# A two-layer diffusion backbone: the pace at which gate projections are handed out inside windowed attention

## The chip, the cores and the metric

The kernel runs on one core of one Trainium2 chip. The metric is the device time of one execution in microseconds (us). Before the change it is 1504.61 us, the median of 3 runs (1503.4 to 1506.65). Engines are called by their names: TensorE (PE in the profile, with PEld for its weight loads), VectorE (DVE), ScalarE (ACT), GpSimd (POOL) and SyncE (SP), which issues the DMA transfers.

## The reference, cut to what matters

There are 1024 latent tokens and 256 context tokens of width 1024, and two layers. The change lies in the first layer, whose core is this:

```python
def even_layer(hl, hc, w_in, sink, ln_g, ln_b, w_s, b_s, w_out, row, col, need_ctx):
    q, k, v, u, vv, gate = jnp.split(hl @ w_in, EVEN_SPLITS, axis=-1)
    q = rope_2d(q.reshape(B_, S, A_HEADS, A_HEAD_DIM), row, col)       # 8 heads of 64
    k = rope_2d(k.reshape(B_, S, A_KV_HEADS, A_HEAD_DIM), row, col)    # 2 key/value heads
    ...
    a = windowed_sink_gqa(q, k, v, kc, vc, sink)   # window of 128, context keys, a sink logit
    b = chunk_gmlp(gelu(u), gelu(vv), ln_g, ln_b, w_s, b_s)
    y = (jnp.concatenate([a, b], axis=-1) * jax.nn.silu(gate)) @ w_out
    ...                                            # the same for the context tokens
```

After it the stream is x + gate_l * y, a norm follows, and the second layer (multi-head latent attention) begins. All matrix products of this kind are made as three matmuls of numbers split into a high and a low part.

## The kernel before, in words

The program computes tokens in blocks of 128 (8 latent blocks, then 2 context blocks: NT = 10), and projections in groups of 512, 512 and 256 tokens (GROUPS). In the first layer `layer0_in` makes queries and keys, then the values and the gMLP branch, and then two things at once:

- `attention0` is a generator over 20 units, each a block of 128 queries with one key/value head (4 query heads). The context blocks come first (two key blocks of 128), then latent blocks 0 to 7: these have three neighbouring key blocks (two at the ends, so units 4, 5, 18 and 19 have one less) and two context key blocks. It works as a pipeline over iterations n = 0 to 23, in the order of ORDER0 (line 48): `S0 S1 D Q M S2 S3 A1 D D A2 P HV HG S4 U D A3 X I F`. S are the scores of unit n, one key block each, with ScalarE's copy (line 712) and VectorE's running maximum (715, 717). M, P, HV, HG, X and F belong to unit n-1: transposes and reduction of the maximum (723, 725), its spread over the partitions (732, with ScalarE's copy mb, 737), the shift of the scores on VectorE and GpSimd (746, 744), the exponentials (752), their fold (761 to 765). A1, A2, U and A3 belong to unit n-2: P·V (774), in odd iterations the row sums (779), and the store (787 to 791). I inverts the sums of some blocks. At each D the generator yields.
- `dense` is a generator of steps of the gates' projections (eight blocks of 128 gate columns, times three token groups). A step is three chunks of K (nine matmuls) or the last two (six). Gate 7 on the latents is done in eight steps of one chunk for both groups, each freeing one tile h0_c, into which `load_wo` (637) then casts a row block of w_out0; before them `load_wo` has issued the loads. After that `gate_out` (563) applies SiLU (ScalarE's tanh, 185; VectorE, 186), multiplies by the gMLP branch (568) and stores to y_d (570).

At every yield of attention, the loop at 630 takes as many steps of `dense` as RATE asks for; PRE = 3 steps are taken ahead. All this stands in a section in which the order of TensorE, ScalarE, VectorE and GpSimd is the order of the program. SyncE's order is the framework's, and so is that of what comes later, which may be put between attention's instructions. Later comes `layer0_out`: for every block of 128 tokens `front` loads yf from y_d (859), the gate halves from ga_d and the inverses from r0_d, multiplies them (867, 868), casts them to yh and yl, and multiplies by w_out0 (881: tiles b<-h,yh, 48 matmuls of 512 columns); `back` normalises and transposes (901).

The loop that hands out the steps:

```python
for _ in range(PRE):
    next(steps)
for n, _ in enumerate(attention):
    while done < (n + 1) * RATE:
        next(steps, None)
        done += 1
for _ in steps:
    assert False
```

Of the kernel before, what the change touches and what calls it, by code (L numbers as in the profile page):

```python
# [25 lines left out]
EPS = 1e-6  # L26
NEG = -1e30
PTS = 3
RATE = 0.95
PRE = 3  # L30
XB = 8
ADA = ((), (), (3, 7), (3, 7), (3,))
# [21 lines left out]
class Kernel:  # L54
# [257 lines left out]
    def layer0_in(self):  # L312
# [311 lines left out]
        with self.tc.manual_schedule(engines={E.PE, E.Activation, E.DVE, E.Pool}):  # L624
# [5 lines left out]
# [3 lines that stand above are left out]
# [946 lines left out]
```

## Time and profile before

| what | value |
|---|---|
| median of 3 runs | 1504.61 us |
| profiled execution, its own time | 1504.3 us |
| its span from first to last instruction | 1502.5 us |
| TensorE busy in the span | 1439.6 us (96%) |
| VectorE busy | 879.5 us (59%) |
| ScalarE busy | 735.9 us (49%) |
| GpSimd busy | 397.4 us (26%) |
| first score matmul of the first layer's attention | 294.00 us |
| last gate matmul of the first layer | 492.55 us |
| first matmul of its output projection | 515.91 us |

In the timeline a row is: start in us, duration in us, engine, line of the kernel, operation, output<-inputs by the program's names, shapes, number of instructions merged into the row, and in brackets the idle time of that engine just before it with what ended it. TensorE's matmuls are pipelined, so rows overlap, and the cost of one in a stream is the distance from start to start. Helpers record their own lines: L100 to L102 are the three matmuls of any split product, L88 any cast on ScalarE, L96 any subtraction of a high part. What is meant shows in the tile names: b<-h,w_hi are gate projections on the latents, b<-h,yh the output projection.

### The profile page before, as it was taken

What the parts mean: (1) busy time and instruction counts of PE and PEld (TensorE: products, weight loads), DVE (VectorE), ACT (ScalarE), POOL (GpSimd) and SP (SyncE); (2) the same over time, 40 slices, a digit from 0 to 9 for tenths busy, and PEclk for the clock granted to TensorE, in tenths of its full rate; (3) what the DMA queues carried; (4) which work ended last, traced back from release to release, by engine and by line L of the source; (5) the groups of instructions that cost most, each with busy time, mean ns of one, the idle gap of its engine ahead of it and who ended that gap; (6) DMA issues with size and microseconds to landing.
All of it is one profiled execution on the core that took longest, in us unless ns stands there. A gap on an engine that the chain in (4) does not pass through costs nothing.

```text
span 1502.5 us, 23133 instructions
## 1 busy us (share of the span) xinstructions
PE 1439.6 (96%) x8849; PEld 1132.6 (75%) x8849; DVE 879.5 (59%) x1690; ACT 735.9 (49%) x1563; POOL 397.4 (26%) x351
## 2 busy tenths in 40 slices
PE   5999999999999799999998999999999999999998
PEld 3766899777666478879887777777777777776786
DVE  5582124356667877543745766676667666766454
ACT  4422310145567635443435766666666666676321
POOL 4243233223556533232470110011001100124100
PEclk9999999999999999999999999999999999999999
DMA  8557401222214646321231000000000000212241
GB/s 329 230 219 272 136 29 29 85 81 85 72 39 155 188 123 191 130 76 57 71 127 39 24 24 15 25 24 24 15 25 24 24 15 22 71 46 81 96 144 71
DMA packets 83783, 132.64 MB, mean 88 GB/s; under 512 B 7552, under 2 KB 59976, under 8 KB 80600
## 3 DMA queue, kind: packets, MB, share of 16 engines
q1 hardware_dynamic: 83528, 130.91, 25.9%
q8 instruction: 69, 1.13, 0.3%
q14 instruction: 42, 0.34, 0.1%
q10 hardware_dynamic: 144, 0.26, 0.0%
HBM read 99.59 MB, written 31.56 MB: 87 GB/s over the span
## 4 chain that ended last, share of the span: by engine, by line
PE 75%; DVE 9%; ACT 5%; issue 4%; DMA 4%; POOL 2%; SPq 0%; POOLq 0%; DVEq 0%; ACTq 0%
PE acc L1270 9%; PE tm L1252 7%; PE s L100 7%; PE s L101 7%; PE s L102 7%; PE b L100 5%; PE b L101 4%; PE b L102 4%; PE s L1215 3%; PE s L1216 3%; PE s L1217 3%; PE tm L100 2%; PE acc L774 2%; DVE peak L1227 2%; ACT prob L1242 2%
## 5 line engine op out<-in xcount | busy, mean ns | idle before, releaser
L1259 ACT COPY pt<-tm 128x512 f32<-128x512 f32 x192 | 112.4, 585 | 165.7 <-PE tm L1252 165.7
L1252 PE MATMUL tm<-ident,prob 128*128 128x128 f32 x1280 | 178.3, 273 | 7.8 <-ACT pt L1259 2.1
L1252 PEld LDWEIGHTS tm<-ident,prob 128*128 128x128 f32 x1280 | 150.8, 140 | 42.0 <-PE tm L1252 9.5
L1242 ACT ACTIVATE prob<-s,peak 128x1024 f32<-128x1024 f32 x128 | 143.3, 1120 | 38.0 <-DVE peak L1231 29.6
L1227 DVE TENSOR_REDUCE peak<-s 128x1 f32<-128x1024 f32 x128 | 155.0, 1211 | 1.8 <-PE s L1217 1.7
L1270 PE MATMUL acc<-pt,v 128*64 128x256 f32 x1280 | 152.0, 384 | 0.0
L96 POOL TENSOR_TENSOR ql<-pe,qh 32x512 fp32r<-32x512 f32 x32 | 40.7, 1271 | 413.2 <-ACT qh L88 386.2
L1261 DVE COPY pt<-tm 128x512 f32<-128x512 f32 x128 | 87.8, 686 | 79.4 <-PE tm L1252 77.4
L96 POOL TENSOR_TENSOR w_lo<-raw,w_hi 128x512 fp32r<-128x512 f32 (+1 forms) x60 | 74.9, 1261 | 199.0 <-DVE w_hi L90 98.5
L1270 PEld LDWEIGHTS acc<-pt,v 128*64 128x64 f32 x1280 | 86.3, 136 | 49.7 <-issue 9.6
L1215 PE MATMUL s<-kh,qh 96*128 96x512 f32 x256 | 109.2, 426 | 2.5 <-DVE raw L186 1.5
L1216 PE MATMUL s<-kl,qh 96*128 96x512 f32 x256 | 100.9, 394 | 0.0
L1217 PE MATMUL s<-kh,ql 96*128 96x512 f32 x256 | 100.8, 394 | 0.0
L1168 DVE TENSOR_TENSOR ql<-tm,qh 64x256 fp32r<-64x256 f32 x62 | 26.1, 421 | 83.7 <-ACT qh L1166 83.3
L100 PE MATMUL b<-h,yh 128*128 128x512 f32 x160 | 63.8, 399 | 3.7 <-ACT yh L88 2.7
L100 PE MATMUL s<-h,w_hi 128*128 128x512 f32 x160 | 63.9, 412 | 2.2 <-ACT qk L380 2.2
L101 PE MATMUL s<-h,w_hi 128*128 128x512 f32 x160 | 63.7, 398 | 0.3 <-DVE rs_v L125 0.3
L101 PE MATMUL b<-h,yh 128*128 128x512 f32 x160 | 63.3, 395 | 0.0
L102 PE MATMUL s<-h,w_lo 128*128 128x512 f32 x160 | 63.0, 395 | 0.0
L102 PE MATMUL b<-h,yl 128*128 128x512 f32 x160 | 62.5, 391 | 0.0
L1242 ACT ACTIVATE prob<-sx,peak 128x256 f32<-128x256 f32 x128 | 61.0, 477 | 0.6
L1217 PEld LDWEIGHTS s<-kh,ql 96*128 96x128 f32 x256 | 48.0, 188 | 11.2
(469 smaller groups left out, 3733.7 us busy)
## 6 DMA issues: line engine op xcount, KB each, us to landing
wa<-in_w_ada_dram SPq DMA_DIRECT2D x16, 1024.0 KB, 9.1
x<-in_xs_dram SPq DMA_DIRECT2D x20, 512.0 KB, 5.6
raw<-in_w_dram SPq DMA_DIRECT2D x17, 512.0 KB, 3.6
wa<-in_w_adag_dram SPq DMA_DIRECT2D x8, 1024.0 KB, 5.9
raw<-in_w_out_dram SPq DMA_DIRECT2D x10, 512.0 KB, 3.9
yf<-y_d SPq DMA_DIRECT2D x10, 512.0 KB, 5.6
x_d<-x SPq DMA_DIRECT2D x8, 512.0 KB, 4.5
raw<-in_w1g_dram SPq DMA_DIRECT2D x8, 512.0 KB, 3.4
```

What stands on the lines that cost most here:

```text
L96: e.tensor_tensor(lo, src, hi.bitcast(F32), op=ALU.subtract)
L100: mm(out, lhsT=ah, rhs=bh, start=start, stop=False)
L101: mm(out, lhsT=ah, rhs=bl, start=False, stop=False)
L102: mm(out, lhsT=al, rhs=bh, start=False, stop=stop)
L1215: mm(o, lhsT=qh[0:96, q], rhs=kh[0:96, k0:k1], start=True, stop=False)
L1216: mm(o, lhsT=qh[0:96, q], rhs=kl[0:96, k0:k1], start=False, stop=False)
L1217: mm(o, lhsT=ql[0:96, q], rhs=kh[0:96, k0:k1], start=False, stop=True)
L1227: nc.vector.reduce_max(m[:, 0, a:a + 1], banks[n, a], axis=AX.X)
L1242: nc.scalar.activation(probs[n][j][:, TL:T] if c else probs[n][j][:, 0:TL], src, AF.Exp, bias=peaks[n][:, 2, j:j + 1], scale=scale, accum_ ...
L1252: nc.tensor.transpose(tp[:, o * P:(o + 1) * P], probs[n][j][:, k * P:(k + 1) * P], self.ident)
L1259: nc.scalar.copy(dst, src)
L1270: mm(accs[m][64 * e:64 * e + 64, 0:QG], lhsT=self.v4[hp // 2][:, kt, vc:vc + 64], rhs=pts[2 * m + e][:, kt], start=kt == 0, stop=kt == NT - 1)
```

## The change

The constant that sets how many steps of `dense` are taken per yield of attention goes from 0.95 to 0.85. Nothing else differs.

```diff
@@ -26,7 +26,7 @@
 EPS = 1e-6
 NEG = -1e30
 PTS = 3
-RATE = 0.95
+RATE = 0.85
 PRE = 3
 XB = 8
 ADA = ((), (), (3, 7), (3, 7), (3,))
```

## Rows read from the trace of the kernel before

**Rows 1.** Windows: stretch, length, busy PE, PEld, DVE, ACT, POOL, clock, DMA share, GB/s.

```profile
360.00:380.00 20.00, 20.00 (x110) 13.96 (x107) 14.23 (x26) 12.77 (x26) 7.74 (x6) 1.00 0.23 75
...
480.00:500.00 20.00, 16.00 (x86) 10.29 (x86) 16.48 (x23) 17.44 (x31) 15.84 (x10) 1.00 0.28 84
500.00:520.00 20.00, 12.79 (x74) 7.67 (x71) 16.45 (x25) 9.40 (x18) 8.74 (x7) 0.91 0.70 223
520.00:540.00 20.00, 20.00 (x110) 15.31 (x109) 18.53 (x29) 11.33 (x22) 8.52 (x7) 1.00 0.48 137
```

**Rows 2.** TensorE's waits from 300 to 493.5: total us, times, longest us.

```profile
PE s L707 <- ACT pt L712: 3.2, 6, 1.1
PE s L723 <- DVE mx L717: 1.2, 2, 0.8
```

**Rows 3.** TensorE's waits from 493.5 to 516.

```profile
PE s L723 <- DVE mx L717: 4.0, 2, 2.6
PE b L100 <- ACT yh L88: 2.7, 1, 2.7
PE tm L732 <- DVE peak L726: 2.6, 1, 2.6
PE s L707 <- ACT pt L712: 0.7, 2, 0.5
```

**Rows 4.** Timeline of TensorE around the last gate step.

```profile
492.32 0.39 PE L101 MATMUL b<-h,w_hi 128*128 128x512 f32 x1
492.55 0.40 PE L102 MATMUL b<-h,w_lo 128*128 128x512 f32 x1
...
499.10 2.38 PE L774 MATMUL acc<-pt,vt 128*64 128x256 f32 x20
504.11 0.65 PE L732 MATMUL tm<-ident,peak 128*128 128x128 f32 x4 [2.63 <-DVE peak L726]
...
505.16 0.64 PE L779 MATMUL acc<-fold,ones 128*32 128x256 f32 x8
...
515.91 0.79 PE L100 MATMUL b<-h,yh 128*128 128x512 f32 x1 [2.74 <-ACT yh L88]
```

**Rows 5.** Windows of the hole, of its end, and of what follows.

```profile
493.05:515.91 22.86, 12.79 (x83) 6.74 (x81) 18.92 (x28) 14.08 (x26) 14.43 (x9) 1.00 0.59 187
512.50:515.91 3.41, 0.67 (x9) 0.15 (x3) 3.38 (x4) 1.10 (x2) 1.68 (x1) 1.00 1.09 372
...
515.91:519.33 3.42, 3.42 (x10) 2.56 (x10) 3.39 (x7) 0.89 (x2) 0.00 (x0) 0.50 0.93 262
```

**Rows 6.** Timeline of ScalarE in the hole.

```profile
495.65 2.27 ACT L752 ACTIVATE pt<-pt 128x512 f32<-128x512 f32 x4 [0.56 <-DVE pt L746]
...
498.77 1.09 ACT L185 ACTIVATE gg<-b 128x512 f32<-128x512 f32 x2
...
507.33 2.27 ACT L752 ACTIVATE pt<-pt 128x512 f32<-128x512 f32 x4 [0.32 <-DVE pt L746]
```

**Rows 7.** Timeline of VectorE: the gates' products and yf's.

```profile
500.23 1.35 DVE L568 SCALAR_TENSOR_TENSOR gg<-gg,ub 128x512 f32<-128x512 f32 x1
502.21 1.04 DVE L568 SCALAR_TENSOR_TENSOR gg<-gg,ub 128x512 f32<-128x512 f32 x1
...
512.37 0.69 DVE L867 SCALAR_TENSOR_TENSOR yf<-yf,raw 128x512 f32<-128x512 f32 x1 [3.27 <-DMA yf<-y_d]
513.09 1.64 DVE L868 TENSOR_TENSOR yf<-yf,raw 128x512 f32<-128x512 f32 x1
```

**Rows 8.** The chain of waits, 485 to 530: start, us, what.

```profile
506.28 5.97 DMA yf<-y_d
```

**Rows 9.** Timeline of TensorE: maxima of three units, one after the other.

```profile
445.96 0.60 PE L723 MATMUL s<-ident,mx 128*128 128x128 f32 x4
...
457.12 0.60 PE L723 MATMUL s<-ident,mx 128*128 128x128 f32 x4
...
468.63 0.66 PE L723 MATMUL s<-ident,mx 128*128 128x128 f32 x4 [0.80 <-DVE mx L717]
```

## The prediction

> **What bounds the kernel now.** TensorE is the busiest engine by far in the page's summary, so I looked for the time that it loses near the edit. The table of 20 us windows over the first layer's attention [rows 1] shows where: from 360 to 380 us the engine is busy 20.00 of 20.00, it loses 4.00 and 7.21 in the two windows from 480 to 520, and nothing in the next. The list of TensorE's waits [rows 2] says that from 300 to 493.5 they come to 4.4 us, in eight pieces: 3.2 for ScalarE's copy of a score block, 1.2 for a maximum on VectorE. From 493.5 to 516 [rows 3] they are 4.0, 2.7, 2.6 and 0.7.
>
> The timeline of TensorE [rows 4] tells what this hole is. The last gate matmul starts at 492.55 and its slot ends at about 493.0. The next matmul that isn't attention's is the first of the output projection (b<-h,yh) at 515.91, 22.9 us later. In between only attention's own matmuls are there, each unit waiting for its own softmax: TensorE was busy 12.79 of 22.86 us, idle 10.07 [rows 5]. From 515.91 the output projection covers the rest of attention.
>
> Why 22.9 us? The projection reads rows of y_d that the last gate block writes, so a chain stands between them. ScalarE has an earlier unit's exponentials and two copies ahead of the gates' tanh, which starts at 498.77 [rows 6], 5.7 us after the last gate matmul. VectorE's four operations on the two gate tiles end at 503.25 [rows 7], 4.5 us. The store must land before SyncE issues the load yf<-y_d at 506.28, 3.0 us, and the load takes 5.97 [rows 8]. Two products on VectorE and a cast on ScalarE lead to 515.91, 3.7 us.
>
> **What the change does to the order.** Attention hands out gate steps at four points D in each of its iterations. Step d, counted from 1 after the three taken ahead, goes to the first point n with (n+1)·RATE > d-1. Steps 1 to 54 are gates 1 to 6, the next three gate 7 on the context, 58 to 65 gate 7 on the latents, one chunk of K each with the w_out0 casts; 66 is gate_out and 67 the closing. At 0.95 step 65 falls on n=67, the last D of iteration 16, and 66 on n=68, the first D of iteration 17. At 0.85 they fall on n=75, the last D of iteration 18, and n=76, the first of iteration 19, where the last unit's scores stand. So the change does what it says. No matmul, copy or transfer is added or removed. Points left empty before the last step were n=19, 39 and 59; now they are 6, 13, 19, 26, 33, 39, 46, 53, 59, 66 and 73, never a first D.
>
> TensorE's work is the same, and the projection is bound by TensorE as soon as it runs [rows 1]. So the change in time is the change in TensorE's idle time, in two places.
>
> **Part 1, the hole** moves; it doesn't go away, since its length is the chain's. The tanh again stands behind the five exponentials of a unit with five key blocks and two copies. I keep 22.9 us less 0.6: VectorE's casts of w_out0 rows made the exponentials wait 0.56 us [rows 6], and one of them has moved a point earlier. So 22.3 us.
>
> What changes is how much attention is left to fill it. Before, the hole held iteration 17 and most of 18: 12.79 us. Now it holds 19 and part of 20, after which there are no scores. Prices from [rows 4]: a score matmul 0.23 from start to start, as two gate matmuls at 492.32 and 492.55 (nine for unit 19's four key blocks, 2.1); the transposes of a maximum 0.4 and those of a spread 0.6; P·V of unit 17 2.4 (20 matmuls); row sums 0.6; then unit 19's maximum 0.4, P·V of unit 18 1.9 (16 of those matmuls), the last spread 0.6. The sum is 9.0 us. Can P·V of unit 19 join? Unit 18's spread would come 11.1 us into the hole, as the one at 504.11 did. From that one to the end of its exponentials at 509.6 took 5.5 us [rows 4, 6]. So P·V of unit 18 runs from 16.6 to 18.5, the last spread ends at 19.1, and P·V of unit 19 could start at 24.6, after the hole. Idle: 22.3 - 9.0 = 13.3 against 10.07, **+3.2 us**.
>
> Bounds. Below: VectorE's slow products (1.35 and 1.04 on the gates, 1.64 on yf) come down to the 0.69 of yf's first product [rows 7]: -2.0, the hole 20.3, its idle 11.3, +1.2. Above: VectorE works in order, and it sat idle for 3.27 us with the yf product at its head [rows 7] while a maximum of attention stood behind it. If that falls ahead of unit 18's or 19's maximum, P·V of unit 18 and the last spread (2.5 us) leave the hole: +5.7. I take the value between, because the chain was measured whole.
>
> **Part 2, shorter iterations.** Iterations 0 to 16 now get 58 steps instead of 65, 0.4 of a step less in each. A full step is nine matmuls of 0.23, 2.0 us; the steps of the context and the last of each three are shorter, so on average an iteration loses 0.6 us of work that hid the softmax. How much cover is needed: from one maximum to the next it took 11.16 us without a wait (445.96 to 457.12) and 11.51 with waits, 0.80 of it for the last maximum (457.12 to 468.63) [rows 9]. The first has gate steps of 3.7 us, the second of 3.1. So with steps under some 3.7 us per iteration the chain of ScalarE and VectorE begins to show, at about 11 us. At the new rate iterations 9, 15 and 16 have 3.4, 3.7 and 3.4 us of steps, the others from 8 to 17 4.4 and more. I take a third of a microsecond for each of the three, and the waits of [rows 2] as staying: +1.0. Bounds: -1.1 (the longest wait in [rows 2], in iteration 16 among the casts that now move to 18, doesn't return, and the floor never binds) and +3.5.
>
> **The clock.** The granted clock was 0.50 from 515.91 to 519.33, the 1.2 GHz level; in the 3.4 us before, TensorE was busy 0.67 us [rows 5]. At full speed the same matmuls take half of 3.42, so 1.7 us were lost. The new hole ends as emptily, so I take no change, and one more such stretch, +1.7, as the upper bound. The Trainium skill, TensorE: Matmul & The Clock Gate, section HAM oscillation, says that idle gaps inside a kernel bring the slow clock back each time, which speaks against thinning out the tail; by it two gaps in the new hole make two slow stretches, and the sum would be +5.9 instead of +4.2. The trace agrees so far as one such gap and one slow stretch [rows 5] can show it.
>
> **Sum.** 3.2 + 1.0 = +4.2 us on the profiled execution's own 1504.3 us (span 1502.5 and 1.8 around it; the median shown is 1504.61, 0.3 above): **1508.5 us**. Its own range is 1505.5 to 1512, from 1.2 to 5.7 of part 1 with the clock's 1.7.
>
> **Rivals.**
> Filled, faster. The waits of iterations 17 and 18 without the last, 7.3 us [rows 3], are filled by the moved steps (eight of six matmuls, 1.36 us each), and the new hole closes, because at attention's end the other engines and the transfers are nearly free. To come out 4 us below before, the chain has to fall to 22.3 - 8.2 = 14 us. Time: 1504.3 - 4 = 1500. For it: VectorE and ScalarE do have less to do in iterations 19 to 21. Against it: of the chain only the 5.7 us ahead of the tanh are queueing, behind work that stays; the rest are its own links. The Trainium skill, Perfetto Trace Analysis, Optimization Strategy, advises to interleave regimes with different limits, which is this rival; taken alone it would give all 7.3 us back, 1497. The trace agrees where gate steps lie between the scores: 20.00 busy of 20.00 [rows 1].
> Even. The hole is at its lower bound and the wait of 1.1 us doesn't return: 1504.3 + 1.2 - 1.1 = 1504.4.
> Floor. The chain of ScalarE and VectorE binds in all eight iterations that newly miss a step (1, 3, 6, 8, 11, 13, 16, 18), at about 1 us each, besides the hole: 1504.3 + 3.2 + 8 = 1515.5. Against it: the early units have two to four key blocks, and [rows 1] shows no idle time in 360 to 380.
> What comes after attention, and SyncE's queue throughout, are ordered by the framework and not by hand; they can shift by a microsecond or two either way, which all ranges hold.
>
> **Chances.** Forecast 0.48, floor 0.08, even 0.29, filled 0.15. About 0.2%, 3.0 us, is what a measurement of this kernel can tell from no change. Slower by more: 0.56; within: 0.29; faster by more: 0.15. The range runs from the filled case's 1500 to the floor's 1515. With 4.2 us so near the bound, "even" is the near miss.
>
> **What would show it.** Right: the waits up to 510 are gone; the last gate matmul ends near 506, and the first b<-h,yh comes 22 to 23 us later, near 528.5; TensorE is idle 12 to 15 us in between, for VectorE's peak and ScalarE's yh; small waits for ScalarE's copies in iterations 9, 15 and 16; one stretch at half clock where the projection starts. Wrong: the distance from the last gate matmul to the first b<-h,yh is under 19 us, or TensorE is busy more than 11 us in it, or the waits before the hole come to more than 8 us.

## The result, and the profile after

With the constant RATE, called the pace from here on, at 0.85 the kernel takes 1513.91 us, the median of 6 runs (1512.95 to 1517.6); the kernel before, run beside it, took 1504.39 (1503.4 to 1506.65). The ratio is 1.0065, with a 95% interval of 1.0055 to 1.0075: 9.5 us slower. The forecast was slower by 4.2, 1508.5 in a range of 1500 to 1515; the forecast's own range was 1505.5 to 1512. The profiled execution of the changed kernel took 1512.95 us, 8.65 above that of before.

The page's summary for the kernel after (engine, busy us, share of the span, instructions) shows the same work in a longer span:

```profile
span 1511.1 us, 23138 instructions
...
PE 1441.2 (95%) x8849; PEld 1131.4 (75%) x8849; DVE 881.0 (58%) x1690; ACT 736.5 (49%) x1563; POOL 395.8 (26%) x351
```

TensorE issues 8849 matmuls, as before, and is busy 1.6 us longer, while the span grew by 8.6. So the time is nearly all idle time of TensorE, as the prediction assumed; the question is where. TensorE's waits of the kernel after (total us, times, longest us), first from 300 us to the last gate matmul, which lies at 507.50 now, to be held against [rows 2]:

```profile
PE s L707 <- ACT pt L712: 3.3, 6, 1.3
PE s L723 <- DVE mx L717: 2.5, 3, 1.3
PE tm L732 <- DVE peak L726: 0.9, 1, 0.9
```

That is 6.8 us (the rows are rounded) against 4.4. Then from there to the first b<-h,yh, where [rows 3] had 10.1:

```profile
PE tm L732 <- DVE peak L726: 3.1, 2, 2.2
PE s L707 <- ACT pt L712: 2.8, 1, 2.8
PE acc L774 <- ACT pt L752: 2.8, 1, 2.8
PE b L100 <- ACT yh L88: 0.4, 1, 0.4
```

That is 9.1. And in the output projection, from 529.6 to 655 us:

```profile
PE b L100 <- ACT b L887: 4.4, 3, 2.1
PE b L102 <- DVE yl L96: 1.4, 1, 1.4
...
PE s L901 <- DVE x L896: 0.2, 1, 0.2
```

with, in the same stretch of the kernel before (516 to 645 us), after the wait at its start that belongs to the hole, only this:

```profile
PE b L100 <- ACT b L887: 0.9, 1, 0.9
```

Three stretches, three answers: before the hole +2.4, in the hole -1, behind it +5. The largest is where the prediction's sum has no term. The 20 us windows of the kernel after (columns as in [rows 1]) show the same, and below them the parts of the hole and of its end, as in [rows 5]:

```profile
500.00:520.00 20.00, 13.88 (x83) 8.14 (x83) 16.68 (x23) 12.74 (x23) 13.45 (x9) 0.95 0.27 86
520.00:540.00 20.00, 14.51 (x64) 9.86 (x61) 14.38 (x22) 7.93 (x14) 7.72 (x6) 0.80 0.90 269
580.00:600.00 20.00, 17.50 (x84) 13.89 (x83) 11.67 (x22) 8.00 (x18) 3.36 (x4) 1.00 0.43 134
600.00:620.00 20.00, 17.92 (x84) 14.71 (x83) 12.76 (x30) 9.03 (x24) 6.21 (x6) 1.00 0.64 207
507.50:529.57 22.07, 12.98 (x73) 7.05 (x71) 15.08 (x24) 11.59 (x22) 12.11 (x8) 0.81 0.47 152
517.85:521.26 3.41, 3.17 (x16) 1.64 (x16) 2.87 (x6) 1.17 (x2) 1.28 (x1) 0.50 0.35 126
521.26:524.68 3.42, 0.77 (x8) 0.56 (x10) 1.70 (x4) 2.29 (x5) 0.74 (x1) 1.00 0.77 221
524.68:531.50 6.82, 5.47 (x21) 2.83 (x17) 2.91 (x6) 1.80 (x3) 3.26 (x3) 0.50 1.05 362
```

Three things to see. In 580 to 620 us, well inside the output projection, TensorE loses 4.6 us at full clock. From the last gate matmul to the first b<-h,yh it is 22.07 us from start to start (23.35 before), and TensorE is busy 12.98 of them, although less work lies there. And the granted clock is 0.50, the 1.2 GHz level, in two stretches near the hole's end, 10.2 us together where there were 3.4.

The timeline of TensorE through the hole (columns as in [rows 4]):

```profile
507.50 0.39 PE L102 MATMUL b<-h,w_lo 128*128 128x512 f32 x1
...
512.71 0.50 PE L707 MATMUL s<-qs,kh 128*128 128x512 f32 x1 [2.75 <-ACT pt L712]
...
517.98 1.11 PE L732 MATMUL tm<-ident,peak 128*128 128x128 f32 x4 [2.23 <-DVE peak L726]
...
523.91 2.98 PE L774 MATMUL acc<-pt,vt 128*64 128x256 f32 x16 [2.75 <-ACT pt L752]
527.79 1.11 PE L732 MATMUL tm<-ident,peak 128*128 128x128 f32 x4 [0.90 <-DVE peak L726]
...
529.57 0.79 PE L100 MATMUL b<-h,yh 128*128 128x512 f32 x1 [0.45 <-ACT yh L88]
...
533.02 0.50 PE L102 MATMUL b<-h,yl 128*128 128x512 f32 x1 [1.39 <-DVE yl L96]
```

The 16 matmuls of P·V took 2.98 us at half clock; at full clock 20 of them took 2.38 [rows 4]. So busy time in the hole is no measure of the work in it. The better one counts its matmuls at their distance from start to start at full clock: 0.227 us for a score matmul or the mask's, 0.119 for one of P·V, 0.11 for a transpose, 0.071 for one of the row sums. The hole of before then holds 11.5 us of work (18 score matmuls, 3 of the mask, 40 of P·V, 13 transposes, 8 of row sums) and that of after 8.8 (8, 1, 36, 17 and 8). What a hole loses is its length less this: 23.35 - 11.52 = 11.83 before, 22.07 - 8.76 = 13.31 after.

**The account.** With this the loss can be written as four terms, for every kernel that was profiled: TensorE's waits between first score and last gate matmul; the hole's length less its work; the waits in the 125 us behind the first b<-h,yh; and half of the time at half clock, outside the hole, in the gates' part and those 125 us (at most that much is lost, since TensorE isn't busy in all of it). One slow stretch of 3.4 us at the first score, which all twelve kernels have, is left out of it. Before: 4.4 + 11.8 + 0.9 + 1.7 = 18.8. After: 6.8 + 13.3 + 6.0 + 1.0 = 27.0. The difference, 8.2, is nearly all of the 8.65 us between the two profiled executions. The same sums are used for the experiments (times in us; the last column is the profiled execution's time less the sum, which would be constant if the account missed nothing):

| kernel | median | ratio (95%) | gates' waits | hole's length | hole's loss | projection's waits | clock | sum | profiled | rest |
|---|---|---|---|---|---|---|---|---|---|---|
| before, pace 0.95 | 1504.4 | 1 | 4.4 | 23.4 | 11.8 | 0.9 | 1.7 | 18.8 | 1504.3 | 1485.5 |
| after, 0.85 | 1513.9 | 1.0065 (1.0055, 1.0075) | 6.8 | 22.1 | 13.3 | 6.0 | 1.0 | 27.0 | 1512.9 | 1485.9 |
| pace 0.90 | 1508.9 | 1.0026 (1.0017, 1.0035) | 6.5 | 23.8 | 12.9 | 0.6 | 0 | 20.0 | 1506.8 | 1486.8 |
| pace 1.0 | 1506.9 | 1.0014 (1.0005, 1.0024) | 2.6 | 24.1 | 11.4 | 6.3 | 0 | 20.3 | 1506.5 | 1486.2 |
| low pace early only | 1505.5 | 1.0002 (0.9993, 1.0012) | 4.9 | 23.5 | 12.0 | 1.8 | 0 | 18.7 | 1506.5 | 1487.9 |
| 0.95, store next to its step | 1508.8 | 1.0023 (1.0013, 1.0032) | 4.4 | 19.0 | 11.2 | 4.4 | 3.4 | 23.4 | 1507.2 | 1483.8 |
| banks, 0.85 | 1511.1 | 1.0050 (1.0035, 1.0065) | 6.8 | 22.5 | 13.7 | 1.4 | 4.3 | 26.1 | 1510.8 | 1484.7 |
| banks, 0.95 | 1503.5 | 0.9996 (0.9987, 1.0006) | 4.4 | 23.5 | 12.0 | 0 | 1.5 | 17.9 | 1501.5 | 1483.6 |
| banks, 1.0 | 1503.9 | 0.9995 (0.9986, 1.0005) | 2.6 | 24.3 | 11.6 | 3.2 | 0 | 17.4 | 1504.3 | 1486.9 |
| banks, 1.1 | 1519.4 | 1.0106 (1.0091, 1.0121) | 3.7 | 25.5 | 11.5 | 13.0 | 8.5 | 36.8 | 1519.9 | 1483.1 |
| filler matmuls, 0.85 | 1512.9 | 1.0048 (1.0034, 1.0061) | 6.8 | 22.3 | 13.6 | 3.9 | 3.4 | 27.6 | 1514.1 | 1486.5 |
| filler matmuls and banks, 0.85 | 1511.1 | 1.0041 (1.0029, 1.0054) | 6.8 | 21.7 | 13.0 | 2.3 | 3.4 | 25.5 | 1511.1 | 1485.5 |

The sums go from 17.4 to 36.8, the rest stays within 4.8 us. So the account carries the large differences; differences below some 5 us between two kernels it doesn't settle, and that 8.2 and 8.65 agree so closely is in part luck. It also stands on one execution of each kernel. For the kernel after, for 0.90 and for the banks at 0.95 that execution was the fastest of all, 1.0, 2.1 and 2.0 us below the median.

**Where the projection waits.** ScalarE's timeline in the kernel after shows the second of the three waits for L887, 1.90 us at 589.93:

```profile
584.38 1.14 ACT L88 CAST w_hi<-raw 128x512 fp32r<-128x512 f32 x2 [2.14 <-issue]
585.43 1.05 ACT L88 CAST yh<-yf 128x1024 fp32r<-128x1024 f32 x1
586.38 2.89 ACT L903 ACTIVATE hf<-s,sT,aT 128x128 f32<-128x128 f32 x8
589.13 0.63 ACT L887 ACTIVATE b<-x 128x512 f32<-128x512 f32 x1
```

and VectorE's the third, 2.08 us at 610.83:

```profile
607.15 0.69 DVE L867 SCALAR_TENSOR_TENSOR yf<-yf,raw 128x512 f32<-128x512 f32 x1 [1.90 <-DMA yf<-y_d]
607.76 0.69 DVE L885 TENSOR_TENSOR b<-b,gate_bc 128x512 f32<-128x512 f32 x1
...
609.29 0.68 DVE L886 TENSOR_TENSOR x<-x,b 128x512 f32<-128x512 f32 x1
```

A tile b lies in a bank of PSUM, the memory into which this kernel's matmuls write. It is free for the next product only when ScalarE has squared it (L887), and only two such banks exist. ScalarE and VectorE work in order. In the first case ScalarE stands for 2.14 us at a cast of w1g, a weight block of a later stage, whose load was issued only at 580.87 (the row names no releaser); yh and eight hf come next, and only then the square that frees the bank. In the second VectorE stands for 1.90 us at the product on yf, whose load hasn't landed, and L885 and L886 of the finished block are behind it. So a transfer that is wanted for later work can stop TensorE, by way of a bank that isn't released. The 1.4 us for yl at the projection's start come about in the same way: VectorE stood at the next block's yf ahead of the first block's yl.

```profile
530.06 0.69 DVE L867 SCALAR_TENSOR_TENSOR yf<-yf,raw 128x512 f32<-128x512 f32 x1 [1.67 <-DMA yf<-y_d]
530.67 2.30 DVE L96 TENSOR_TENSOR yl<-yf,yh 128x1024 fp32r<-128x1024 f32 x1
```

Not every such stand costs something. In the kernel after VectorE also stood 3.99 us at the yf product of 596.88, and TensorE waited no more than 0.18 us near it; in the kernel before VectorE stood three times for 1.8 to 2.5 us at yf in the projection, with 0.9 us of waits in all. What counts is what stands behind the late instruction. The kernel before has the same cast of w1g, with ScalarE standing 1.40 us at it, but the square comes directly behind it, and the 0.92 us that TensorE waits there are its only wait for L887:

```profile
581.24 1.14 ACT L88 CAST w_hi<-raw 128x512 fp32r<-128x512 f32 x2 [1.40 <-DMA raw<-in_w1g_dram]
582.28 0.59 ACT L887 ACTIVATE b<-x 128x512 f32<-128x512 f32 x1
```

The Trainium skill, Perfetto Trace Analysis, section Optimization Strategy, reads a gap that keeps coming back on the busiest engine as a possible lack of space in SBUF or PSUM for the next tile. Three gaps for the same release in 28 us agree with it; the bank experiments below tried it.

### The profile page after: what moved, and what is told of

Its sections match the earlier page's. It is cut to its first block, busy times and chain, and to the rows that moved or that the text cites. A ratio compares the mean times of both kernels' runs of the same rounds, so it can differ in the third digit from the quotient of the medians.

```text
span 1511.1 us, 23138 instructions
## 1 busy us (share of the span) xinstructions
PE 1441.2 (95%) x8849; PEld 1131.4 (75%) x8849; DVE 881.0 (58%) x1690; ACT 736.5 (49%) x1563; POOL 395.8 (26%) x351
## 4 chain that ended last, share of the span: by engine, by line
PE 77%; DVE 10%; ACT 4%; issue 4%; DMA 3%; POOL 1%; SPq 0%; POOLq 0%; DVEq 0%; ACTq 0%
PE acc L1270 9%; PE s L100 7%; PE s L101 7%; PE s L102 7%; PE tm L1252 7%; PE b L100 4%; PE b L102 4%; PE b L101 4%; PE s L1215 3%; PE s L1216 3%; PE s L1217 3%; PE acc L774 2%; PE tm L100 2%; DMA yf<-y_d 2%; DVE peak L1227 2%
## 5 line engine op out<-in xcount | busy, mean ns | idle before, releaser
L1168 DVE TENSOR_TENSOR ql<-tm,qh 64x256 fp32r<-64x256 f32 x62 | 26.1, 421 | 83.8 <-ACT qh L1166 83.4
```

## The experiments

**Half of the step: pace 0.90.** Does the loss grow with the pace?

```diff
-RATE = 0.95
+RATE = 0.90
```

> The constant is 0.90, halfway. The last gate step (65) falls on the last D of iteration 17, gate_out on the first D of 18. Theory: the change's 9.5 us are three terms, read off the two traces: waits of TensorE up to the last gate step (before 4.4 us, with 0.85 6.8 us and some 1.5 us that no wait row shows), the hole from the last gate matmul to the first b<-h,yh with its slow clock (lost time 10.1 against 12.8), and the output projection that has less attention left between its matmuls (waits after its first matmul before 2.2 us, with 0.85 7.2 us). At 0.90 the hole holds iteration 18 and iteration 19 up to its P.V, about 10.3 us of attention in 22: lost 11.7. So +1.6 for the hole, about +1 for the pace, +1 to +3 for the projection: 1508 to 1510. Rival, the hole and its slow clock alone: 1506. Rival, a chance order of the projection's instructions made by the framework: no order in the times, 1504 and 1514 both possible.

Measured: 1508.94 us, ratio 1.0026 (1.0017 to 1.0035), +3.9. The last gate matmul starts at 501.79, between the two others. The waits before it are 6.5 us, as many as at 0.85 already; the hole's loss is 1.0 above before; the projection waits 0.6. The projection's 5 us come with 0.85, then, and not with every lower pace. The time lies in the expected range, but not by the expected terms: the projection, with 1 to 3 us the largest of them, gave nothing in this execution (-0.3). The pace and the hole give 3.2 by the account, less 1.7 for a slow stretch that isn't there. Since this execution was the fastest of ten, 2.1 us below the median, no trace shows the rest of the 3.9.

**The other direction: pace 1.0.** If more attention left over for the projection is what spares TensorE its waits, a higher pace should be faster than before.

```diff
-RATE = 0.95
+RATE = 1.0
```

> The constant is 1.0. The last gate step falls on the first D of iteration 16, gate_out on the second D of the same iteration. Theory: waits of TensorE up to the last gate step fall from 4.4 to 3 us or less, the hole is covered by units with five key blocks (lost time 9 to 10, as before), the projection has more attention left between its matmuls, so waits after its first matmul stay at 2 us or less: 1501 to 1504. Rival, the hole alone: 1504. Rival, a chance order: anything from 1500 to 1510.

Measured: 1506.85 us, ratio 1.0014 (1.0005 to 1.0024): slower than before, where the theory said faster. The pace does what it should before the hole (2.6 us of waits) and in it (11.4). But the projection waits 6.3 us, although 15.5 us of attention's matmuls lie behind its start (11.8 before, 2.6 after). TensorE's waits from 512 us on, in this kernel:

```profile
PE b L100 <- ACT b L887: 4.0, 2, 2.1
PE tm L732 <- DVE peak L726: 1.6, 1, 1.6
PE acc L774 <- ACT pt L752: 0.7, 1, 0.7
```

4.0 us are again for L887. The theory that attention's leftover covers the projection falls: the same wait comes with little of it and with much. In this kernel too ScalarE stood 3.28 us at the cast of w1g shortly before the first of the two waits, and VectorE 2.23 us at a yf product before the second. By these timelines, what differs from pace to pace is which late casts and products stand ahead of a bank's release.

**Thin early, end as before.** Up to iteration 11 the pace is 0.85, then it catches up, and from point 60 on it is that of before. This takes the shorter iterations without the late end.

```diff
-                while done < (n + 1) * RATE:
+                while done < ((n + 1) * 0.85 if n < 48 else 41 + (n - 47) * 16 / 12 if n < 60 else (n + 1) * RATE):
```

> The pace is 0.85 up to iteration 11 and then 16 steps are handed out at 12 points, so that from iteration 15 on every step stands where it stands before the change. Only the early thinning is left. Theory: the waits of TensorE in iterations 1 to 11 come as with 0.85 (2.9 us there against 1.6 before), hole and projection as before: 1505 to 1507. If thinning cost more than its waits show (the 1.5 us in no wait row), 1507 to 1508. Rival, the end alone makes the loss: 1504.

Measured: 1505.54 us, ratio 1.0002 (0.9993 to 1.0012). The early waits of the kernel after are there, 0.91 for a peak and 0.80 and 0.53 for ScalarE's copies, and yet the waits before the hole come to 4.9 us, 0.5 above before: where the steps are denser later, the waits of iterations 14 and 15 (1.7 us before) are gone, and one of 1.1 us for a bank of the gates is new. The time shows no loss beyond its interval, which ends at +1.8 us. So the early thinning, made good by a catch-up, isn't what costs the 9.5 us. Thin late iterations and a late end remain; this run doesn't tell them apart.

**Shorten the chain.** At 0.95, the last step of gate 7 hands over to `gate_out` without going back to attention, so that tanh and store come a point earlier.

```diff
                 if c >= WLAG:
                     next(wo)
-                yield
+                if c < KC - 1: yield
```

> The constant is 0.95. The yield between the last gate step and gate_out is taken out, so gate_out's tanh stands directly behind the last gate matmuls on ScalarE, ahead of five exponentials and two copies, and everything else as before. Theory: the hole is as long as its chain, and the 5.7 us between the last gate matmul and the tanh are queueing; they shrink to 1 us, the first b<-h,yh comes 17 to 19 us after the last gate matmul instead of 23.4 (starts), the hole's lost time falls from 10 to 6: 1500 to 1502. Rival: the tanh and VectorE's four gate operations (4.5 us) delay the exponentials and the shift of the units in flight by as much, the hole is no shorter: 1504 to 1506.

Measured: the hole is 19.01 us, 4.3 shorter, as expected. The time is 1508.76, ratio 1.0023 (1.0013 to 1.0032), slower, where faster was expected. With the length the work in the hole fell, from 11.5 to 7.8 us, so its loss fell by 0.6 only. The projection began before what feeds it was ready (2.2 us for yh, 1.6 for yl, 2.1 for L887, where before had 2.7 for yh, none for yl and 0.9 for L887), and the clock was at 0.50 in 498.1 to 504.9 and again in 511.7 to 518.6, the second time in the projection. So here the shorter chain was no gain by itself: it moved the projection's start ahead of work that still had to be done.

**A free bank for the projection, 0.85.** From block 3 on, the second half of the output projection takes its PSUM tile from the rotating set of four that the transposes use, so that a late L887 no longer stops it.

```diff
-                ps.append(self.psum("b", 2))
+                ps.append(self.bank() if h and t > 2 else self.psum("b", 2))
```

> The constant is 0.85, and from the fourth token block on the output projection's second half goes to one of the four PSUM banks that attention has given back, instead of the second of its own two. Theory: with 0.85 TensorE waits 4.4 us in three pieces for ScalarE to release a bank (b <- ACT b L887), because ScalarE or VectorE, which work in order, stand with a cast of the next weights or a product of yf at their head whose transfer has not landed, and the release is queued behind. With more banks these three waits go and nothing else: 1509 to 1510.5 against 1513.9 for 0.85 alone. Rival, cover: with attention gone from between the projection's matmuls, the loads of yf themselves are late; then the waits turn into waits for yh or yl (b <- ACT yh, b <- DVE yl) of the same size: 1512.5 to 1514.

Measured: 1511.08 us (1510.7 to 1512.86, 4 runs), ratio 1.0050 (1.0035 to 1.0065). In the list of TensorE's waits from 531 to 655 us the three waits for L887 are gone:

```profile
PE b L102 <- DVE yl L96: 1.4, 1, 1.4
```

That shows what the 4.4 us were. The median fell by 2.8 us only, between the two forecasts, and the intervals of the two ratios overlap. In the profiled execution the clock took back a part:

```profile
525.80:530.90 5.10, 3.19 (x15) 1.50 (x11) 1.42 (x3) 1.09 (x2) 1.66 (x2) 0.50 1.08 361
530.90:539.40 8.50, 7.11 (x16) 5.14 (x17) 8.00 (x11) 3.96 (x7) 2.21 (x2) 0.50 0.84 244
```

Here the slow clock lasted through the first 8.5 us of the projection, where the kernel after had 1.9. Half of the difference, 3.3 us, is lost in this one execution. The medians that doesn't explain: the mean granted clock over all runs is 0.990 here and 0.989 in the kernel after. Why the median fell by less than the waits stays open.

**The same at other paces.** Is 0.85 slower because of the banks alone?

> The constant is 0.95, with the same banks for the projection. Control: before the change only one such wait of 0.92 us stands in the trace. Theory: 1503.5 to 1504.5. If the banks shift the order of the framework in some other way: outside of 1502.5 to 1505.5.

> The constant is 1.0, with the same banks for the projection. With 1.0 alone the way to the last gate step is 2.8 us cheaper than before, counted with the attention work that is left, and the projection 5.7 dearer, of which 4.0 us are two waits for a bank. Theory: these 4.0 go, 1502.5 to 1504 against 1506.85. Rival, cover: 1506 to 1507, as there is more attention left between the projection's matmuls than before and it did not help.

> The constant is 1.1, with the same banks. The last gate step falls on iteration 14, gate_out one point later. Theory: still fewer waits up to the last gate step (2 us or less), a hole over iterations 15 and 16 with five key blocks each, no waits for a bank: 1500 to 1504. If packing more gate work into each iteration buys nothing, since work moved ahead only leaves a longer bare stretch, 1504 to 1507.

Measured: at 0.95 1503.49 (ratio 0.9996, 0.9987 to 1.0006), at 1.0 1503.88 (0.9995, 0.9986 to 1.0005), at 1.1 1519.42 (1.0106, 1.0091 to 1.0121). With the banks freed the loss that 1.0 had over 0.95 is gone, so that loss was the release of banks too (the waits for L887 went from 4.0 us to none). Between 0.95 and 0.85 there are still 7.6 us. So by the medians the banks explain 2 to 3 us of the 9.5; by the account the rest is the gates' waits (2.4), the hole (1.7), the wait for yl (1.4) and the clock (2.8), and no experiment took these away one by one. At 1.1 the expectation failed by 15 us. Its waits from 475 us on:

```profile
PE s L901 <- ACT hf L903: 6.0, 2, 5.3
PE s L723 <- DVE mx L717: 5.6, 2, 4.2
PE b L102 <- DVE yl L96: 5.0, 2, 3.7
```

There the projection starts with 24 us of attention's matmuls still to come, and waits of other kinds take their place, with 17 us at half clock. The 5.3 us are of the known kind: VectorE stood 6.15 us for the load of x at the sum with it (L886, 586.46 us), and ScalarE's squares, a cast of w1g and hf followed one after the other.

**Keep the clock up in the hole.** 35 matmuls (bf16, 512 columns) that nobody needs stand in the idle places of the hole: 10 ahead of the fourth scores of unit 19, 8 and 6 ahead of the spreads of units 18 and 19, 11 ahead of P·V of unit 18. They write to tiles that are overwritten afterwards. `warm(t, c)` issues c of them into tile t; its definition isn't shown.

```diff
...
-            kt = keys(n)[j]
+            kt = keys(n)[j]; (n, j) == (19, 3) and (accs.update({17: self.psum("acc")}), warm(accs[17], 10))
...
-            tp = self.psum("tm")
+            tp = self.psum("tm"); warm(tp, {18: 8, 19: 6}.get(n, 0))
...
-            if a == 0:
-                accs[n] = self.psum("acc")
+            if a == 0 and n not in accs:
+                accs[n] = self.psum("acc"); warm(accs[n], 11 * (n == 18))
```

> The changed kernel with 35 extra bf16 matmuls of 512 columns on TensorE in the idle places of the hole: 10 ahead of the fourth scores of unit 19, 8 and 6 ahead of the spreads of units 18 and 19, 11 ahead of P.V of unit 18. They write into tiles that are overwritten afterwards. Nothing else waits for them, so the chain from the last gate matmul to the first b<-h,yh should stay at 22 us (21.5 to 23). Theory 'clock has a price of its own': the stretches at 0.50 between 517.85 and 531.50 go or shrink to one, the slow time per run falls from 33 us to 21 to 27, and the time falls by half of the 5.5 us that TensorE was busy in 524.68:531.50 and up to that much again, to 1510 (1509.5 to 1512). Rival 'the hole is as long as its chain, and what the clock slows there lies in idle time': the clock goes to 1.00 in the hole, but its length stays and the time is 1513 to 1514.5.

> The same extra matmuls on the kernel at 0.85 whose second half of the output projection takes a PSUM bank that is free (e5: 1511.08, with 525.8 to 539.4 at the slow clock, TensorE busy nearly throughout). Theory 'clock': that stretch goes, which gives back half of its 13.6 us less what one stretch of 3.4 at the projection's start still costs: 1506 to 1508.5. Rival 'length of the hole's chain': at most 1 us, 1510 to 1511.5.

Measured: 1512.87 us, ratio 1.0048 (1.0034 to 1.0061) without, 1511.06, ratio 1.0041 (1.0029 to 1.0054) with the free banks. The windows of the first of the two, of the hole and of the one slow stretch behind it:

```profile
510.45:532.76 22.31, 17.93 (x107) 8.84 (x105) 15.06 (x24) 11.59 (x22) 12.13 (x8) 1.00 0.46 152
537.55:541.00 3.45, 3.45 (x10) 2.67 (x9) 3.45 (x6) 2.57 (x5) 0.06 (x1) 0.51 1.04 279
```

The clock was 1.00 through the whole hole, TensorE was busy 17.93 us in it, and its length is 22.31 where it was 22.07. So what the half clock slowed in the hole lay in time that was idle anyway; the hole's length is the chain's, as the rival said. With the free banks it was 21.73. The slow clock came later instead, at 537.6, and with the free banks from 533.5 to 540.3, in both cases in the projection, soon after a wait of 2.3 us for yl. In the first of the two another slow stretch of 3.4 us, at 466.0, lies in the gates' part, where the kernel after has none. The medians are 1.0 us below the kernel after and equal to the banks alone; the intervals of the ratios overlap. The clock of all runs says more than one trace: its mean is 0.994 with the added matmuls and 0.989 in the kernel after, which makes some 19 and 34 us of half clock per run (an estimate: twice the missing share of the run). So about 15 us less of it went with a median 1.0 us lower, or 2 us lower when each is set against the kernel before run beside it, which took 1505.41 here. 1512.87 lies between the forecasts of the two theories: for the hole's length the rival is shown right, while for the time a price of the clock of 1 to 2 us isn't excluded.

In this kernel the projection has its own two banks again, and ScalarE and VectorE stand at the cast of w1g and at the yf product nearly as long as in the kernel after (2.10 and 1.85 us). Yet the waits for L887 are 1.5 us and not 4.4. So at one and the same pace their size changes with small shifts in time.

## Why the prediction was right, and where it was not

The direction, the place of the new hole and its length came out as forecast; the size did not, +4.2 where +9.5 came. That the time lies in the stated range is in good part luck. The terms that the sum holds came to +3.2 in the traces (1.5, 2.4 and -0.7 below), and the other 5 us from a place without a term. 1513.91 is above the forecast's own range, which ends at 1512, and the 1515 that covers it comes from the rival "floor", whose mechanism the runs don't show. That own range also leaves out part 2; with the bounds of part 2 it would have been 1504.4 to 1515.2. By its steps:

**The order.** The last gate matmul starts at 507.50 and the first b<-h,yh at 529.57; forecast were an end near 506 and 528.5.

**The hole's length: right, partly by balance.** From where TensorE fell free of gates to the first b<-h,yh 21.84 us, forecast 22.3. The single links differ from the forecast's. The tanh starts 5.3 us after the last gate matmul's slot (forecast 5.7 less 0.6), VectorE ends 4.1 later (4.5). These rows are ScalarE's, then VectorE's:

```profile
513.04 1.09 ACT L185 ACTIVATE gg<-b 128x512 f32<-128x512 f32 x2
...
528.47 1.04 ACT L88 CAST yh<-yf 128x1024 fp32r<-128x1024 f32 x1 [4.50 <-DVE yf L868]
```

```profile
516.09 1.05 DVE L568 SCALAR_TENSOR_TENSOR gg<-gg,ub 128x512 f32<-128x512 f32 x1
...
526.97 0.69 DVE L867 SCALAR_TENSOR_TENSOR yf<-yf,raw 128x512 f32<-128x512 f32 x1 [2.24 <-issue]
527.58 0.15 DVE L726 TENSOR_TENSOR peak<-stA,sink 128x4 f32<-128x4 f32 x1
```

From there to the issue of the load it took 4.7 us instead of 3.0. SyncE's queue shows the reason (DMA issues in its order):

```profile
515.48 2.01 SPq L570 DMA_DIRECT2D y_d<-gg  x2
519.33 0.80 SPq L308 DMA_DIRECT2D gate_bc<-gate_d  x2
520.82 0.37 SPq L788 DMA_DIRECT2D y_d<-ot  x1
521.23 0.54 SPq L791 DMA_DIRECT2D s_d<-ot  x1
521.81 0.44 SPq L130 DMA_DIRECT2D yf<-y_d  x1
```

Attention's own store (788, 791) stands ahead of the load now, and waits for ScalarE's copy of ot. In return the load took 5.2 us instead of 5.97, and the last links 2.6 instead of 3.7. The risk that the yf product on VectorE would fall ahead of a maximum came true for unit 19, whose peak (L726) ran at 527.58, right behind the product. It cost nothing that counts, since only the last spread stood behind it.

**The hole's loss: over-sized, by a mixed measure.** Forecast were 9.0 us of work and 13.3 idle, +3.2. The work was 8.8. But +3.2 set that work, at prices from start to start, against the 12.79 busy us of the window of before; by one measure for both it is 13.3 - 11.8 = +1.5. The two marks that the prediction set for itself, idle 12 to 15 us and busy no more than 11, weren't met either (9.09 and 12.98), because half clock stretched the same matmuls; the second is one of its own signs of being wrong. With the clock kept up, the same hole had 17.93 - 8.23 = 9.7 busy us of attention (8.23 for the four groups of added matmuls in its timeline), which leaves some 12.6 of its 22.31 us idle without them, inside the first mark.

**The shorter iterations: under-sized.** +2.4 instead of +1.0, inside the bounds of -1.1 to +3.5. The places were wrong as well. Iteration 15 has a wait of 1.34 us, but for VectorE's maximum, and 9 and 16 have none of note. 0.85 and 1.26 us are in iterations 17 and 18, which the prediction took to be covered by the steps that move there ("the waits up to 510 are gone"); the longest wait of before, 1.15 us in iteration 16, went along with the casts to iteration 18. The early ones (0.91, 0.80, 0.53) are real, but the experiment with the low pace early only shows no price beyond its interval for that thinning.

**The projection: the step that failed.** "The projection is bound by TensorE as soon as it runs" was read from one window of 20 us in its beginning [rows 1]. It holds for before, with 0.9 us of waits in 125. At the new pace they are 6.0 in the profiled execution, +5.05, the largest term: 4.4 for PSUM banks, 1.4 for yl and 0.2 for a transpose. By the medians the banks' part is 2 to 3 us. The prediction did say that SyncE's queue and the later order could shift "by a microsecond or two either way"; it priced what it couldn't see at nothing and its bound at less than half of what came. That the 4.4 us are the banks' release is shown by the edit that removes them. The load of w1g comes no later for the projection than before: it is issued 51.3 us behind the first b<-h,yh, where it was 61.7 before (577.64), and 9.2 us fewer of attention's matmuls lie behind that first one. What differs is the order on ScalarE, where yh and eight hf now stand between the late cast and the square; that order is the framework's, and why it comes out so was not tried.

**The clock.** Taken as 0 with +1.7 as the bound. Around the hole the slow time grew from 3.4 us to 10.2, in two stretches with a gap of 3.4 us ahead of the second in which TensorE was busy 0.77. The two stretches are what the Trainium skill, TensorE: Matmul & The Clock Gate, section HAM oscillation, made the prediction name as its other sum, +5.9. The trace agrees with the stretches, but not with that price: 8.3 of the 10.2 us lie in the hole, whose length didn't change when the clock was kept at 1.00, and in the projection the profiled execution had less slow time than before (1.9 against 3.4 us, -0.7). In other executions there is more: the mean granted clock over the six runs of the kernel after was 0.986 to 0.992, 0.992 in the profiled run, which is the fastest, and 0.986 in the slowest, 1517.6. So the clock can make much of the 1 us between the profiled run and the median, though this is argued and no trace shows where.

**The sum.** Forecast 3.2 + 1.0 = +4.2; measured in the traces 1.5 + 2.4 + 5.05 - 0.7 = +8.2 of 8.65.

**The rivals.** "Filled" fell: the waits didn't close, and at 1.0, the opposite direction, the hole's loss was 11.4 against 11.8 and not larger. "Even" fell with the interval. "Floor" gave a time near the measured one, 1515.5, by a mechanism that isn't there: eight iterations with a microsecond each would make 8 us of new waits before the hole, and there are 2.4.

## What to carry to other kernels

A pace for filler work moves everything behind it as well: look at the stage that follows for engines that work in order and hold a scarce buffer, since a late transfer at their head can stop TensorE through the buffer that isn't released. Price a hole by its length less its work at one fixed price per matmul, never by busy time, which half clock stretches. And shortening or filling a hole pays only if what follows it is ready: here a chain 4.3 us shorter made the kernel slower, and a full clock in the hole made it faster by no more than the noise.

## What the runs showed of the hardware

The granted clock stayed at 0.50 for 13.6 us in one kernel (525.8 to 539.4), through 8.5 us in which TensorE was busy 7.11; in others the slow stretch ended after 3.4, 6.8 or 10.2. Matmuls of 512 columns then started 0.42 to 0.43 us apart (530.16, 530.58 and 531.01 in the kernel after) instead of 0.23. With matmuls added only to keep the engine busy the clock was 1.00 where they stood (22.31 us), and a slow stretch came after the next long wait behind them instead (2.3 us, then 3.4 and 6.8 at half clock).

A VectorE subtraction on 128x1024, yl, took 2.30 us at 530.67, at the projection's start, and 1.22 at 587.44. GpSimd was busy for 1.22 of the 2.30 us and ScalarE for none; in the shorter one ScalarE was busy throughout and GpSimd not at all. At 611.75 it took 1.23 with the DMA engines busy all the time (a share of 1.02). So neither ScalarE nor the transfers alone lengthen it. GpSimd beside it may, but not each time: at pace 1.0 (546.1 us) it took 1.22 with GpSimd busy for 95% of it.
